# Carrying the extra tokens of a split-precision projection as trailing columns of one matmul

## The chip, the core and the metric

The kernel runs on one core of one Trainium2 chip. The metric is the device time of one launch in microseconds (us): 1000.98 us before the change, the median of 3 runs (1000.5 to 1001.47).

## What is computed

One layer of a hybrid encoder over 512 tokens with 16 learned meta tokens ahead of them, so 528 token columns. Cut to what matters here:

```python
h_res = concat([meta(16), x(512)])            # (528, 2048)
P = rmsnorm(h_res, g) @ w_in                  # w_in: 2048 x 8320
Pr, Pc = P[:, :4224], P[:, 4224:]
Pr = Pr + (shift_by_one_token(Pr) - Pr) * mu  # r, k, v, g_r and two low-rank inputs
y_a = rwkv7(r, decay, k, v, kk, a) ...        # recurrence over all 528 tokens
Bg, Cg, hc, g_c = split(Pc)
y_b = Bg * causal_conv_width3(Cg * hc) * silu(g_c)
out = rmsnorm(h_res + concat([y_a, y_b]) @ w_out)[16:]
```

The output keeps only the 512 real tokens. k and v enter the recurrence, which starts at the meta tokens, so they need all 528 columns. r, g, C and h need the 512 real tokens and the two tokens before them (token shift, convolution). B and g_c need the 512 alone.

## The kernel before, in words

Every float32 operand of the projection is split into a high and a low part of type fp32r, `x = xh + xl` and `w = hi + lo`, and a product is the sum of three matmuls: hi by xh, hi by xl, lo by xh. The tokens lie along the free dimension: `xh` and `xl` are 128 partitions by 16 slices of the 2048 inputs (`KT`) by `LX` = 576 columns, of which the first 528 hold tokens.

The projection is cut into 65 tiles of 128 output columns, in the order of `plan`: the low-rank tile, then 8 each of k, r, v, g, B, C, h and gc. A tile's weights arrive by DMA in four quarters; ScalarE rounds each to its high part (L158) and VectorE or GpSimd forms the low part (L159). `main` (L358) makes a tile with `steps` (L337): for each quarter, for each of the token ranges, for each of the quarter's 4 slices, three matmuls into one PSUM bank. The ranges are

```python
FULL = ((0, 272), (272, L))     # k, v, low-rank: 272 and 256 columns, two banks
TAIL = ((14, 272), (272, L))    # r, g, C, h: 258 and 256 columns, two banks
REAL = ((META, L),)             # B, gc: 512 columns, one bank
```

so a FULL or TAIL tile is 96 matmuls (48 of each width) and a REAL tile 48. The first four tiles (low-rank, k0, r0, B0) run interleaved while the inputs still arrive; of the tiles after them 15 are FULL (k1 to k7 and the eight v) and 31 are TAIL (r1 to r7 and the eight each of g, C and h).

A finished tile is evacuated by `scaled` (L371): VectorE multiplies each bank by `rs`, the row of RMS factors of the tokens, into an SBUF tile (`pr`, or `u` and `hh` for C and h). `shift_full` and `shift_real` then apply the token shift: ScalarE scales the tile by mu (`sh`), VectorE adds the rest.

TensorE's order is written out by hand. `mains` is a generator that yields after every matmul with a modelled time of 0.43 ns a column; `fill(ns)` emits projection matmuls until so many modelled ns have gone by, `until` emits them until a given tile is done. Between the fills stand the blocks of the recurrence's preparation: `prepare(i)` waits for k and r of head pair i, makes decay-scaled operands `ar` and `bk` on VectorE, then after `fill(FW["gram"])` the Gram matmuls (L703, and L713 for the meta chunk) that read them. `FW` is the table of these fills; `gram` holds for even i. `recur` does the same for the nine steps of the recurrence later. The other engines' order is made by a scheduler from the program's dependencies. After the projection follows the output product (L1285) in a form with seven block products, and the final norm.

Of the kernel before, what the change touches and what calls it, by code (L numbers as in the profile page):

```python
# [9 lines left out]
F32 = mybir.dt.float32  # L10
# [3 lines left out]
ALU = mybir.AluOpType  # L14
# [26 lines left out]


FW = dict(
    evac=34, start=1062, lora=2200, gram=8000, meta={0: 2000}, gram_b=13500, gram2=5500, misc=2000, v=2000, vt=1000, solve=24500, more={0: 5500, 2: 2400},
    tr=3200, lev=3000, cp=4200, out=1500, begin=19500, p=2900, u=2900, s=5200, last=3700, mix=2600,
)

# [51 lines left out]
def hymba_kernel(ctx: ExitStack, tc: tile.TileContext, xt, xtok, front, w_in, w_out, pv, lup, cst, msk, gf, out):  # L99
# [77 lines left out]
    xh = xp.tile([P, KT, LX], F32R, name="xh")  # L177
    xl = xp.tile([P, KT, LX], F32R, name="xl")
    rs = xp.tile([P, L], F32, name="rs")
    la = cq.tile([P, 2, L], F32R, name="la")  # L180
    ones = xp.tile([P, P + 2], F32R, name="ones")
    omm = xp.tile([P, 33], F32, name="omm")
# [150 lines left out]
    FULL = ((0, 272), (272, L))  # L333
    TAIL = ((14, 272), (272, L))
    REAL = ((META, L),)

    def steps(ps, ranges, k4, q, ks=range(4), rs_=range(2)):  # L337
        hi, lo = quarters[q]
# [12 lines left out]
    def banks(ranges, name, pool, tag):  # L351
        return [pool.tile([P, b - a], F32, tag=tag, name=f"ps_{name}_{r}") for r, (a, b) in enumerate(ranges)]
# [5 lines left out]
    def main(j, ranges, name):  # L358
        prefetch(2 * j + 4)
        early = state["banks"]  # L360
        state.update(tile=j, step=0, banks=[])
        ps = [early[r][:, 0 : b - a] for r, (a, b) in enumerate(ranges)] if early else banks(ranges, name, pm, "main")
        for k4 in range(4):
            if k4 == 1:
                prefetch(2 * j + 5)
            for t in steps(ps, ranges, k4, 4 * j + k4):
                state["step"] += 1
                yield t
        return ps

    def scaled(ranges, ps, dst, base):  # L371
        for (a, b), p in zip(ranges, ps):
            nc.vector.tensor_tensor(out=dst[:, a - base : b - base], in0=p, in1=rs[:, a:b], op=ALU.mult)

# [116 lines left out]
    def token_scale(yb, part):  # L491
        prs = pi.tile([P, 512], F32, tag="misc", name="prs")
        if part == 0:
            for j in range(4):
                nc.tensor.transpose(prs[:, j * P : (j + 1) * P], yb[:, j], ident)
            nc.vector.tensor_copy(rs[:, 0:512], prs)
        else:
            nc.tensor.transpose(prs[:, 0:META], yb[0:META, 4], ident[0:META, 0:META])
            nc.vector.tensor_copy(rs[:, 512:L], prs[:, 0:META])

    def mains():
        pa = banks(FULL, "lora", pm, "main")
        pb = banks(FULL, "k0", pz, "tz")
        pc = banks(TAIL, "r0", pm, "main")
        pd = [pi.tile([P, SEQ], F32, tag="ser", name="ps_B0")]
        four = ((pa, FULL), (pb, FULL), (pc, TAIL), (pd, REAL))
        for k in range(4):
            for n, (ps, rg) in enumerate(four):
                if k == n == 0:
                    hi, lo = quarters[0]  # L510
                    for ww, xx, first in ((hi, xh, True), (lo, xh, False), (hi, xl, False)):
                        for p, (a, b) in zip(ps, rg):
                            nc.tensor.matmul(p, ww[:, 0:P], xx[:, 0, a:b], start=first, stop=False)
                            yield (b - a) * 0.43
                    continue
                yield from steps(ps, rg, 0, 2 * n, (k,))
        for k4 in range(1, 4):
            for n, (ps, rg) in enumerate(four):
                h = 4 * (k4 // 2) + n
                if k4 == 2:  # L520
                    prefetch(h + 3)
                if (k4, n) == (3, 3):
                    for ks, part in ((range(1), 0), (range(1, 3), 4), (range(3, 4), None)):
                        yield from steps(ps, rg, k4, 2 * h + k4 % 2, ks)
                        if part is not None:
                            token_scale(yb, part)
                        if part == 4:
                            use("lora", 0, pa)
                            use("k", 0, pb)
                    continue  # L530
                for r in range(2 if n < 3 else 1):
                    if (k4, n, r) == (3, 1, 1):
                        yb = token_scale_sums()
                    yield from steps(ps, rg, k4, 2 * h + k4 % 2, range(4), (r,))
        use("r", 0, pc)
        use("B", 0, pd)
        for j in range(4, len(plan)):
            what, i = plan[j]
            rg = FULL if what in ("k", "v") else REAL if what in ("B", "gc") else TAIL
            ps = yield from main(j, rg, f"{what}{i}")  # L540
            if (what, i) == ("h", 0):
                state["conv"] = low[4 * j + 6]
            if what == "gc" and i < 4:
                state["split"] = low[4 * j + 4]
            use(what, i, ps)
# [1022 lines left out]
```

## Time and profile before

| | |
|---|---|
| median of 3 runs | 1000.98 us (1000.5 to 1001.47) |
| the profiled execution, its own time | 1001.71 us |
| its span on the core | 999.9 us |
| granted TensorE clock, mean | 0.997 |
| TensorE matmuls: busy, instructions | 988.3 us, 9723 |
| VectorE busy | 685.7 us |
| ScalarE busy | 394.6 us |
| GpSimd busy | 271.5 us |

The profiled execution lasted 1.8 us longer than its span, for what lies around the program. A matmul's start is recorded and its end modelled: neighbouring matmuls overlap in the records, so what a matmul costs in a stream is the distance from one start to the next, not its listed duration. In the chain of work, a row gives the start, the length and the count of a stretch of equal work.

### The profile page before, as it was taken

How to read it: one execution, taken by the hardware profiler on the slowest of the kernel's cores; microseconds unless marked ns; L12 is line 12 of the kernel's file. 1: busy time of each engine (PE TensorE's matmuls, PEld its weight loads, DVE VectorE, ACT ScalarE, POOL GpSimd, SP SyncE). 2: the span in 40 equal slices, each digit the busy share in tenths (PEclk: the TensorE clock that was granted, in tenths of full speed). 3: DMA queues.
4: the chain of work that ended last, by engine and by line, in shares of the span. 5: the costliest groups of instructions: out<-in, count | busy, mean ns of one | idle time of the engine just before them, and what ended most of it. 6: DMA issues, size and time to landing. Idle time of an engine off the chain costs nothing.

```text
span 999.9 us, 23699 instructions
## 1 busy us (share of the span) xinstructions
PE 988.3 (99%) x9723; PEld 911.6 (91%) x9723; DVE 685.7 (69%) x1247; ACT 394.6 (39%) x729; POOL 271.5 (27%) x292
## 2 busy tenths in 40 slices
PE   9999999999999999999999999999999999999996
PEld 7999999999998999998999998889889898888885
DVE  6777965588765679744669644244554697997897
ACT  7553433344313434322434322222232426546463
POOL 0122423234233424232324222223332333001001
PEclk9999999999999999999999999999999999999998
DMA  9525576555575373854274846877673688797654
GB/s 329 148 85 148 132 207 171 153 144 145 141 189 165 95 193 98 203 149 119 85 197 108 197 136 192 297 215 241 204 226 99 174 264 210 187 318 175 160 127 168
DMA packets 185036, 174.82 MB, mean 175 GB/s; under 512 B 121568, under 2 KB 142816, under 8 KB 184416
## 3 DMA queue, kind: packets, MB, share of 16 engines
q1 hardware_dynamic: 182336, 164.40, 57.2%
q0 software_dynamic: 2304, 8.39, 4.8%
q8 instruction: 76, 1.25, 0.5%
q10 hardware_dynamic: 288, 0.52, 0.1%
q14 instruction: 32, 0.26, 0.1%
HBM read 136.92 MB, written 36.35 MB: 173 GB/s over the span
## 4 chain that ended last, share of the span: by engine, by line
PE 90%; DVE 5%; DMA 2%; issue 1%; SPq 0%; ACT 0%; POOL 0%; DVEq 0%; ACTq 0%; POOLq 0%
PE ps_v L346 9%; PE ps_k L346 9%; PE ps_h L346 9%; PE ps_g L346 9%; PE ps_r L346 9%; PE ps_B L346 9%; PE ps_gc L346 9%; PE ps_C L346 8%; PE M L1285 5%; PE P L1285 2%; DVE o L1256 2%; PE g L703 2%; PE Q L1285 1%; PE zs L1048 1%; PE ps_lora L346 1%
## 5 line engine op out<-in xcount | busy, mean ns | idle before, releaser
L158 ACT CAST w<-wr 128x512 fp32r<-128x512 f32 x252 | 153.0, 619 | 285.4 <-PE ps_C L346 47.3
L159 POOL TENSOR_TENSOR w<-wr,w 128x512 fp32r<-128x512 f32 x119 | 169.1, 1422 | 346.6 <-ACT w L158 289.4
L159 DVE TENSOR_TENSOR w<-wr,w 128x512 fp32r<-128x512 f32 x133 | 98.6, 747 | 114.5 <-ACT w L158 114.2
L346 PE MATMUL ps_k<-xh,w 128*128 128x272 f32 (+1 forms) x512 | 95.3, 284 | 0.0
L346 PE MATMUL ps_v<-xh,w 128*128 128x256 f32 (+1 forms) x512 | 95.3, 284 | 0.0
L346 PE MATMUL ps_r<-xh,w 128*128 128x258 f32 (+1 forms) x512 | 94.4, 281 | 0.0
L346 PE MATMUL ps_h<-xh,w 128*128 128x256 f32 (+1 forms) x512 | 94.0, 282 | 0.0
L346 PE MATMUL ps_C<-xh,w 128*128 128x256 f32 (+1 forms) x512 | 93.1, 281 | 0.0
L346 PE MATMUL ps_g<-xh,w 128*128 128x256 f32 (+1 forms) x512 | 91.5, 280 | 0.0
L346 PE MATMUL ps_B<-xh,w 128*128 128x512 f32 x256 | 83.8, 395 | 0.0
L346 PE MATMUL ps_gc<-xh,w 128*128 128x512 f32 x256 | 81.3, 392 | 0.0
L346 PEld LDWEIGHTS ps_k<-xh,w 128*128 128x128 f32 x512 | 80.0, 188 | 0.4
L346 PEld LDWEIGHTS ps_v<-xh,w 128*128 128x128 f32 x512 | 80.0, 188 | 0.3
L346 PEld LDWEIGHTS ps_h<-xh,w 128*128 128x128 f32 x512 | 79.2, 188 | 0.7
L346 PEld LDWEIGHTS ps_r<-xh,w 128*128 128x128 f32 x512 | 79.6, 188 | 0.1
L346 PEld LDWEIGHTS ps_C<-xh,w 128*128 128x128 f32 x512 | 79.2, 188 | 0.6
L346 PEld LDWEIGHTS ps_g<-xh,w 128*128 128x128 f32 x512 | 78.7, 188 | 0.2
L346 PE MATMUL ps_k<-xl,w 128*128 128x272 f32 (+1 forms) x256 | 72.6, 284 | 0.0
L346 PE MATMUL ps_v<-xl,w 128*128 128x272 f32 (+1 forms) x256 | 72.5, 283 | 0.0
L346 PE MATMUL ps_h<-xl,w 128*128 128x258 f32 (+1 forms) x256 | 71.8, 281 | 0.5 <-issue 0.5
L346 PE MATMUL ps_g<-xl,w 128*128 128x258 f32 (+1 forms) x256 | 72.0, 281 | 0.0
L346 PE MATMUL ps_r<-xl,w 128*128 128x258 f32 (+1 forms) x256 | 72.0, 281 | 0.0
(337 smaller groups left out, 2265.3 us busy)
## 6 DMA issues: line engine op xcount, KB each, us to landing
wr<-in_w_in_dram SPq DMA_DIRECT2D x126, 512.0 KB
ct<-opd SPq DMA_DIRECT2D x64, 288.0 KB
wo<-in_w_out_dram SPq DMA_DIRECT2D x24, 512.0 KB
x<-in_w_out_dram POOLq DMA_DIRECT2D x16, 512.0 KB, 6.1
opd<-ar SPq DMA_DIRECT2D x8, 576.0 KB
opd<-gt SPq DMA_DIRECT2D x16, 288.0 KB
opd<-bt SPq DMA_DIRECT2D x64, 64.0 KB
x<-in_w_out_dram SPq DMA_DIRECT2D x8, 512.0 KB
```

The costliest lines, as they stand in the source:

```text
L158: nc.scalar.copy(hi, rq)
L159: low[q] = eng.tensor_tensor(out=lo, in0=rq, in1=hi.bitcast(F32), op=ALU.subtract).ins
L346: nc.tensor.matmul(ps[r], ww[:, w], xx[:, kt, a:b], start=(kt == 0 and n == 0), stop=(kt == KT - 1 and n == 2))
L703: nc.tensor.matmul(z[h][:, c - c0], bk[hs, c, h : h + 2, :].rearrange("p a s -> p (a s)"), ar[hs, c].rearrange("p a s -> p (a s)"), start= ...
L1048: nc.tensor.matmul(d[hs, j], w, x[hs], start=(a == 0), stop=(a == b - 1))
L1256: last = nc.vector.tensor_tensor(out=lo, in0=rq, in1=hi.bitcast(F32), op=ALU.subtract)
L1285: nc.tensor.matmul(bank[s], left(prod, jj, m, s), w, start=(jj == 0 and n == 0), stop=(jj == 7 and n == 2))
```

## The change

Two token ranges of 256 columns take the place of the two ranges of FULL and TAIL in every such tile after the first four. The tokens ahead of the 512 (16 for k and v, 2 for the others) are no longer columns of the first range. Their high and their low parts are copied once, by ScalarE, behind the 528 columns of `xh`: first the high parts of tokens 14 and 15, then their low parts, then the high and the low parts of tokens 0 to 13. The second range's matmuls read over its end into them:

| per slice of the inputs | before, FULL | after, "full" | before, TAIL | after, "tail" |
|---|---|---|---|---|
| first bank: hi·xh, hi·xl, lo·xh | 272, 272, 272 | 256, 256, 256 | 258, 258, 258 | 256, 256, 256 |
| second bank: hi·xh, hi·xl, lo·xh | 256, 256, 256 | 288, 256, 274 | 256, 256, 256 | 260, 256, 258 |
| columns in all | 1584 | 1586 | 1542 | 1542 |

A matmul of `hi` so makes hi·xh and hi·xl of an extra token in two different columns of the bank, and at the evacuation these are added: VectorE scales the extra columns into a small tile `ex` (with `rsx` or `rst`, the RMS factors in the same column order), GpSimd adds the two halves into the first columns of the destination (one addition for "tail", two for "full"). The number of matmuls, the weights and the rest of the projection stay. `FW["gram"]` goes from 8000 to 8800, which puts the Gram blocks of even head pairs seven matmuls later in TensorE's order.

```diff
-    evac=34, start=1062, lora=2200, gram=8000, meta={0: 2000}, ...
+    evac=34, start=1062, lora=2200, gram=8800, meta={0: 2000}, ...
...
+    rst = xp.tile([P, 4], F32, name="rst")
+    rsx = cq.tile([P, 2 * META], F32, name="rsx")
...
+    HALF, EX = META + SEQ // 2, 2 * META
+    WIDE = {"full": (L + EX, L, L + META + 2), "tail": (L + 4, L, L + 2)}
+
+    def copy_meta():
+        for o, x, a, b in ((0, xh, META - 2, META), (2, xl, META - 2, META), (4, xh, 0, META - 2), (META + 2, xl, 0, META - 2)):
+            nc.scalar.copy(xh[:, :, L + o : L + o + b - a], x[:, :, a:b].bitcast(F32))
+
+    def copy_scale():
+        for o, a, b in ((0, META - 2, META), (2, META - 2, META), (4, 0, META - 2), (META + 2, 0, META - 2)):
+            nc.scalar.copy(rsx[:, o : o + b - a], rs[:, a:b])
+        nc.scalar.copy(rst, rsx[:, 0:4])
+
+    def pieces(kind, ps, k4, q):
+        hi, lo = quarters[q]
+        for r in range(2):
+            a = HALF if r else META
+            ends = WIDE[kind] if r else (HALF,) * 3
+            for k in range(4):
+                kt = 4 * k4 + k
+                w = slice(k * P, (k + 1) * P)
+                for n, (ww, xx, b) in enumerate(((hi, xh, ends[0]), (hi, xl, ends[1]), (lo, xh, ends[2]))):
+                    nc.tensor.matmul(
+                        ps[r][:, 0 : b - a], ww[:, w], xx[:, kt, a:b], start=(kt == 0 and n == 0),
+                        stop=(kt == KT - 1 and n == 2), skip_group_check=True,
+                    )
+                    yield (b - a) * 0.43
...
     def scaled(ranges, ps, dst, base):
+        if len(ranges) == 2 and ps[0].shape[1] == SEQ // 2:
+            n = ps[1].shape[1] - SEQ // 2
+            e = (tp if n == 4 else cq).tile([P, n], F32, tag=f"ex{n}", name="ex", bufs=2)
+            for r, (a, b) in enumerate(((META, HALF), (HALF, L))):
+                if r:
+                    nc.vector.tensor_tensor(out=e, in0=ps[1][:, SEQ // 2 :], in1=rst if n == 4 else rsx, op=ALU.mult)
+                nc.vector.tensor_tensor(
+                    out=dst[:, a - base : b - base], in0=ps[r][:, 0 : b - a], in1=rs[:, a:b], op=ALU.mult
+                )
+            nc.gpsimd.tensor_tensor(out=dst[:, META - 2 - base : META - base], in0=e[:, 0:2], in1=e[:, 2:4], op=ALU.add)
+            if n > 4:
+                nc.gpsimd.tensor_tensor(
+                    out=dst[:, -base : META - 2 - base], in0=e[:, 4 : META + 2], in1=e[:, META + 2 : EX], op=ALU.add
+                )
+            return
...
             nc.vector.tensor_copy(rs[:, 512:L], prs[:, 0:META])
+            copy_scale()
+            copy_meta()
...
-            rg = FULL if what in ("k", "v") else REAL if what in ("B", "gc") else TAIL
+            rg = "full" if what in ("k", "v") else REAL if what in ("B", "gc") else "tail"
```

`main` is changed to take its matmuls from `pieces` where the range is one of the two names.

More of the change, by code (lines that the diff above doesn't have):

```diff
@@ L43 @@
 FW = dict(
-    evac=34, start=1062, lora=2200, gram=8000, meta={0: 2000}, gram_b=13500, gram2=5500, misc=2000, v=2000, vt=1000, solve=24500, more={0: 5500, 2: 2400},
+    evac=34, start=1062, lora=2200, gram=8800, meta={0: 2000}, gram_b=13500, gram2=5500, misc=2000, v=2000, vt=1000, solve=24500, more={0: 5500, 2: 2400},
     tr=3200, lev=3000, cp=4200, out=1500, begin=19500, p=2900, u=2900, s=5200, last=3700, mix=2600,
@@ L361, in main @@
         state.update(tile=j, step=0, banks=[])
+        kind = ranges if isinstance(ranges, str) else None
+        if kind:
+            ranges = ((META, HALF), (HALF, WIDE[kind][0]))
         ps = [early[r][:, 0 : b - a] for r, (a, b) in enumerate(ranges)] if early else banks(ranges, name, pm, "main")
@@ L365, in main @@
                 prefetch(2 * j + 5)
-            for t in steps(ps, ranges, k4, 4 * j + k4):
+            for t in pieces(kind, ps, k4, 4 * j + k4) if kind else steps(ps, ranges, k4, 4 * j + k4):
                 state["step"] += 1
```

## The prediction

> **What bounds the kernel now.** I read the head of the page first, then who TensorE waits for, then the chain of work in order of time, then single matmuls in the timeline.
>
> ```profile
> PE 988.3 (99%) x9723; PEld 911.6 (91%) x9723; DVE 685.7 (69%) x1247; ACT 394.6 (39%) x729; POOL 271.5 (27%) x292
> PE 90%; DVE 5%; DMA 2%; issue 1%; SPq 0%; ACT 0%; POOL 0%; DVEq 0%; ACTq 0%; POOLq 0%
> ```
>
> ```profile
> PE pwarm L207 <- DVE cold L204: 1.4, 1, 1.4
> PE ps_h L346 <- issue: 0.5, 1, 0.5
> PE M L1285 <- DVE o L1256: 0.4, 1, 0.4
> PE ps_lora L346 <- ACT w L247: 0.4, 1, 0.4
> ```
>
> TensorE holds 90% of the chain that ended last, and its four longest waits in the whole span are 1.4, 0.5, 0.4 and 0.4 us. So the time is the sum of the distances between matmul starts, and an edit counts by what it does to these distances. The chain of waits gives them for whole tiles (start, length, count):
>
> ```profile
> 142.20 11.20 PE ps_h L346 x96
> 380.32 11.53 PE ps_v L346 x96
> 782.71 10.88 PE ps_gc L346 x48
> 793.59 11.39 PE ps_C L346 x96
> ```
>
> The REAL tile takes 10.88 / 48 = 226.7 ns for 512 columns. The two-bank tiles mix two widths, which the timeline takes apart. Each row below is the hi·xl matmul of a slice, three matmuls after the one before (start, duration, ...):
>
> ```profile
> 142.16 0.28 PE L346 MATMUL ps_h<-xl,w 128*128 128x258 f32 x1
> ...
> 143.24 0.28 PE L346 MATMUL ps_h<-xl,w 128*128 128x258 f32 x1
> ...
> 143.59 0.28 PE L346 MATMUL ps_h<-xl,w 128*128 128x256 f32 x1
> ...
> 144.61 0.28 PE L346 MATMUL ps_h<-xl,w 128*128 128x256 f32 x1
> ```
>
> ```profile
> 380.29 0.29 PE L346 MATMUL ps_v<-xl,w 128*128 128x272 f32 x1
> ...
> 381.43 0.29 PE L346 MATMUL ps_v<-xl,w 128*128 128x272 f32 x1
> ```
>
> Nine distances each: 1.08 / 9 = 120.0 ns for 258 columns, 1.02 / 9 = 113.3 ns for 256, 1.14 / 9 = 126.7 ns for 272. The tiles agree: 48 x (120.0 + 113.3) = 11.20 us, 48 x (126.7 + 113.3) = 11.52 us. In steps of 6.67 ns these are 17 steps for 256, 18 for 258, 19 for 272 and 34 for 512. Two columns past 256 cost a whole step. A rule that fits all four is 17/16 of a step per 16 columns, rounded up to whole steps: 256 gives 17.0, 258 gives 17.1 and so 18, 272 gives 18.06 and so 19, 512 gives 34.0. That rounding is what the change works on: the columns stay the same in number, but three matmuls per slice that are rounded up become two.
>
> **TensorE, term by term.** By this rule 260 columns take 18 steps (17.3 rounded up), 288 take 20 (19.1), 274 take 19 (18.2).
>
> - Tail, per slice: before 3 x 18 + 3 x 17 = 105 steps; after 4 x 17 + 18 + 18 = 104. One step, 6.67 ns.
> - Full, per slice: before 3 x 19 + 3 x 17 = 108; after 4 x 17 + 20 + 19 = 107. One step again; if 274 should take 20, none.
> - 46 tiles x 16 slices x 6.67 ns = 4.9 us off; with no gain in the 15 full tiles 31 x 16 x 6.67 = 3.3 us.
>
> Not every 256 runs at 113.3 ns. After a foreign block some runs stay slower, and so does a whole tile (ps_C above, 11.39 against 11.20 us, 0.19 us over 48 narrow matmuls, 4 ns each):
>
> ```profile
> 84.53 0.28 PE L346 MATMUL ps_r<-xl,w 128*128 128x256 f32 x1
> ...
> 85.59 0.28 PE L346 MATMUL ps_r<-xl,w 128*128 128x256 f32 x1
> ...
> 985.91 5.91 PE L1494 MATMUL end<-home,m 128*128 128x256 f32 x48
> ```
>
> The first pair gives 1.06 / 9 = 117.8 ns, 4.5 ns more; the last row, the end of the output product, (5.91 - 0.28) / 47 = 119.8 ns. A wide matmul has nothing to lose there, a narrow one has, and the change makes 736 more narrow ones (one more per slice). I take a quarter of them to be slow, an estimate between the clean tiles and ps_C: 736 x 4.5 x 1/4 = 0.8 us. So TensorE's work falls by 4.9 - 0.8 = 4.1 us, between 2.5 (no gain in the full tiles) and 4.9 us.
>
> The Trainium skill, "TensorE: Matmul & The Clock Gate", section "Back-to-back issue gap", makes the isolated distance linear in the columns, N / 2.4 + 2.5 ns when warm. That would be 109.2 and 110.0 ns for 256 and 258, where the trace has 113.3 and 120.0; the measurement decides for the step. By the page's rule the tail tiles would gain nothing and the full ones lose two columns per slice.
>
> **Evacuation.** Prices come from the nearest small instructions (line engine op ... count | busy, mean ns | idle):
>
> ```profile
> L158 ACT CAST w<-wr 128x512 fp32r<-128x512 f32 x252 | 153.0, 619 | 285.4 <-PE ps_C L346 47.3
> L159 POOL TENSOR_TENSOR w<-wr,w 128x512 fp32r<-128x512 f32 x119 | 169.1, 1422 | 346.6 <-ACT w L158 289.4 <-issue 38.6 <-DMA opd<-bt 8.6
> L377 POOL MEMSET pr_k<- 128x1 f32 x8 | 0.8, 100 | 5.4 <-DVE r L391 5.4
> L1084 POOL TENSOR_SCALAR nv<-nv 128x8 f32<-128x8 f32 x8 | 2.7, 332 | 20.4 <-DVE nv L1083 20.0
> L596 ACT ACTIVATE tz<-tz,hv 128x16 f32<-128x16 f32 x8 | 2.2, 275 | 1.3 <-PE tz L593 1.3
> ```
>
> VectorE gets 46 products of 4 or 32 PSUM columns. The 16-column copy of `rs` out of PSUM (0.17 us, row below) is nearest: 46 x 0.17 = 7.8 us on an engine that is busy 69% of the span. GpSimd gets 31 + 2 x 15 = 61 additions of 2 or 14 columns, between 100 ns (a memset of one column) and 332 ns (8 columns read and written). I take 332, the nearer in kind: 20 us on an engine busy 27%. What matters is the new wait: ScalarE's `sh` and, behind it in ScalarE's queue, weight casts now wait for a GpSimd addition, which may stand behind a weight split of 1.42 us. The casts have room: they idle 285.4 us in all, waiting mostly for TensorE to free a weight buffer, and the splits behind the additions on GpSimd idle 346.6 us. VectorE's token shift waits for `sh`. So `ar`, `bk`, `k`, `r` may come 0.3 us later as a rule and up to 0.33 + 1.42 = 1.8 us later at worst. Who waits for them on TensorE are the Gram blocks, and the tightest is this one:
>
> ```profile
> 348.22 0.68 DVE L686 TENSOR_TENSOR ar<-r,e 128x512 f32<-128x512 f32 x1
> ```
>
> ```profile
> 350.18 0.40 PE L713 MATMUL ps_k<-ar,bk 64*128 64x16 f32 x4
> ```
>
> `ar` is done at 348.90, 1.28 us ahead of the block. `gram` at 8800 moves the block seven matmuls later, 0.8 us, which makes 2.1 us, more than the worst hop. That move costs TensorE nothing by itself: the same matmuls stand in another order, and the DMAs that SyncE issues behind the block go 0.8 us later with it. In the recurrence the step that waits for `pn` has this cover:
>
> ```profile
> 661.57 0.66 ACT L1004 ACTIVATE pn<-rz 128x256 f32<-128x256 f32 x2 [2.75 <-PE rz L996]
> ```
>
> ```profile
> 664.86 0.34 PE L1013 MATMUL rz<-pn,ct 64*64 64x64 f32 x8
> ```
>
> 664.86 - 662.23 = 2.6 us, again more than one hop. Without cover a hop would cost its 1.8 us each time. I book 0.4 us for stalls that add up where hops meet, with 0 and 1.8 us as ends.
>
> **Copies.** `copy_meta` is four ScalarE copies. In the built order they stand after the last square of the input and shortly before the weight cast of this row, which idle time precedes:
>
> ```profile
> 37.96 0.62 ACT L158 CAST w<-wr 128x512 fp32r<-128x512 f32 x1 [1.22 <-issue]
> ```
>
> 4 x 0.28 = 1.1 us fits into these 1.22 us: nothing. `copy_scale` is five more, 5 x 0.28 = 1.4 us, from the moment `rs` is whole, ahead of `sh` of the low-rank tile. The first reader on TensorE is the low-rank product of head pair 0:
>
> ```profile
> 53.06 0.17 DVE L499 COPY rs<-prs 128x16 f32<-128x16 f32 x1
> ```
>
> ```profile
> 54.48 0.74 ACT L380 ACTIVATE sh_lora<-pr_lora,pvt 128x528 f32<-128x528 f32 x1
> ...
> 57.94 0.63 ACT L411 CAST la<-lora_al 64x528 fp32r<-64x528 f32 x1
> ```
>
> ```profile
> 60.53 0.29 PE L592 MATMUL tz<-la,luh 128*128 128x272 f32 x1
> ```
>
> `la` is done at 58.57, 1.96 us ahead of use. ScalarE idled before 53.95, so of the copies about 0.7 us reach past it: hidden.
>
> **Sum.** -4.1 + 0.4 = -3.7 us. On the profiled execution that is 1001.7 - 3.7 = 998.0; the median of the runs is 0.7 us lower, so 1000.98 - 3.7 = 997.3 us.
>
> **The rivals.** The rule of steps was seen in runs of 12 equal widths. The second bank now changes its width with every matmul (260, 256, 258), which this trace shows nowhere in a settled stream. Against a price for that: ps_h above changes width eight times and still takes 11.20 us, the sum of its parts. For it: the 256s at 117.8 ns and at 119.8 ns show that a narrow matmul can lose a step to its surroundings.
>
> - The narrow matmul between two wide ones is slow, 117.8 ns throughout: 736 x 4.5 x 3/4 = 2.5 us come back. -4.1 + 2.5 + 0.4 = -1.2, so 999.8 us: no change that can be told.
> - Each change of width costs: of the second bank's three matmuls two lose a step of 6.67 ns. One step per slice is where gain turns to loss; at two, 736 x 2 x 6.67 = 9.8 us against 4.9 us, with the stalls +5.3, so 1006.3 us. This is the case on the slower side.
> - The change does nothing: cost is linear after all, from 113.3 and 226.7 at 0.443 ns a column, and 258 and 272 are dear for another reason that stays. Then the full tiles pay 15 x 16 x 2 x 0.443 = 0.2 us and the stalls 0.4: 1001.6 us. The linear rule of the skill's section above is of this kind; the trace so far speaks against it.
> - 258 and 272 are dear because of the column at which they start (14 and 0, against 272 for the 256s). Then the tail slice would be 4 x 113.3 + 115.1 + 114.2 = 682.5 ns instead of 700.0, and all slices 736 x 17.5 = 12.9 us less: 988.5 us. 272 starts in the same way as 256 in all but the number, so this is unlikely.
>
> **How the numbers follow.** The forecast 0.55, the slow narrow matmul 0.24, the paid width changes 0.14, linear 0.04, the start column 0.03. A measurement of this kernel tells about 0.2%, 2.0 us, from no change: below 999.0 is faster, above 1003.0 slower. Faster: 0.55 + 0.03, less 0.01 for the forecast's own slow edge (2.5 us off and 1.8 us of stalls), 0.57. Within: 0.24 + 0.04 less 0.01, 0.27. Slower: 0.14, and 0.02 for stalls that pile up, 0.16. The range has to hold the forecast's own spread (4.9 us off and no stall, 996.1) and reach to the slow narrow matmul and the linear case, 1001.6: 995.9 to 1001.8. The forecast's case alone would be 996.1 to 999.0.
>
> **What would show it.** In the changed kernel's chain, an undisturbed tail tile (C or h early on) should take 16 x 104 x 6.67 = 11.09 us and a full one 16 x 107 x 6.67 = 11.41. In the timeline the triples of the first bank should be 340 ns, of the second 353 in a tail tile and 373 in a full one. TensorE's waits should stay below 1 us in all behind the start. I am wrong about the steps if the second bank's triple in a tail tile is near 358 (slow narrow) or 367 (paid changes), and wrong about the cover if Gram or recurrence lines appear among TensorE's waits.

## The result, and the profile after

The changed kernel takes 1005.91 us (median of 6 runs, 1004.18 to 1006.27), the kernel before on the same chip 1001.18 us (6 runs, 1000.5 to 1001.55): a ratio of 1.0045, 95% interval 1.0032 to 1.0058. It is slower by 4.7 us, where 3.7 us less were forecast. The profiled execution of the changed kernel lasted 1006.14 us, its span 1004.0 us, against 1001.71 and 999.9 us before.

The head of the page after, the counterpart of the row that the prediction started from:

```profile
span 1004.0 us, 23849 instructions
...
PE 990.3 (99%) x9723; PEld 914.5 (91%) x9723; DVE 692.4 (69%) x1293; ACT 396.3 (39%) x738; POOL 284.7 (28%) x353
```

The matmuls are as many as before, and TensorE still bounds the kernel. VectorE has 6.7 us more work, GpSimd 13.2 us, both with room. Who TensorE waits for in the changed kernel (in total, times, longest):

```profile
PE ps_g L761 <- DVE pr_v L409: 1.9, 2, 1.2
PE pwarm L209 <- DVE cold L206: 1.4, 1, 1.4
PE zy L1100 <- issue: 1.4, 1, 1.4
PE M L1333 <- DVE o L1304: 0.4, 1, 0.4
```

The first row is new. L761 is the meta Gram block (L713 before). It writes into the two PSUM banks that the next tile will use, and waits there for VectorE's products L409 of a v tile, which free these banks. The third row (`zy`, with no releaser that the profile shows) stands at the same place as the 0.5 us of `ps_h` before. The chain of work shows the second part (start, length, count of whole tiles):

```profile
130.68 11.32 PE ps_C L359 x96
142.00 11.36 PE ps_h L359 x96
```

The prediction wanted 11.09 us for such a tile; before it was 11.20. One stretch out of `ps_h`, the hi·xl matmuls of a quarter in the second bank (the first two rows) and then in the first bank of the next quarter:

```profile
143.37 0.28 PE L359 MATMUL ps_h<-xl,w 128*128 128x256 f32 x1
...
144.44 0.28 PE L359 MATMUL ps_h<-xl,w 128*128 128x256 f32 x1
144.80 0.28 PE L359 MATMUL ps_h<-xl,w 128*128 128x256 f32 x1
...
145.85 0.28 PE L359 MATMUL ps_h<-xl,w 128*128 128x256 f32 x1
```

Nine distances each: 1.07 / 9 = 118.9 ns in the second bank (260, 256, 258), 1.05 / 9 = 116.7 ns in the first, where all are 256 and 113.3 was expected. Means of the distance by position over all slices behind the first four tiles, from the starts in the two traces (distances over 150 ns, in which a wait or another block stands, are left out):

| ns | first bank: hi·xh, hi·xl, lo·xh | second bank | per slice |
|---|---|---|---|
| TAIL before | 120.0, 120.2, 120.0 (258) | 114.8, 114.9, 114.6 (256) | 704.3 |
| "tail" after | 117.3, 116.1, 116.7 (256) | 120.8 (260), 117.9 (256), 119.1 (258) | 707.8 |
| FULL before | 126.7, 126.5, 126.7 (272) | 114.1, 113.8, 113.8 (256) | 721.5 |
| "full" after | 116.2, 115.2, 114.6 (256) | 134.8 (288), 116.1 (256), 123.3 (274) | 720.2 |

The wide matmuls cost about what was forecast (120.0, 120.0, 133.3, 126.7). The narrow ones do not: their means are 114.6 to 117.9 ns, where they were 113.8 to 114.9 before and 113.3 was expected. Added up over the 46 tiles, these distances make 522.6 us before and 523.9 us after. I call this sum the TensorE sum below.

So there are two parts: 1.4 us in the TensorE sum, and new waits of which the two at the meta Gram blocks of head pairs 5 and 7 hold most (1.19 and 0.67 us idle; the tiles behind them start 1.7 and 1.1 us later against the trace before, 2.8 us in all); the wait ahead of `zy` is 0.9 us longer than the one at its place before.

### The profile page after: what moved, and what is told of

Read it like the earlier page. It is cut to its first block, busy times and chain, and to the rows that moved or that the text cites. A ratio compares the mean times of both kernels' runs of the same rounds, so it can differ in the third digit from the quotient of the medians.

```text
span 1004.0 us, 23849 instructions
## 1 busy us (share of the span) xinstructions
PE 990.3 (99%) x9723; PEld 914.5 (91%) x9723; DVE 692.4 (69%) x1293; ACT 396.3 (39%) x738; POOL 284.7 (28%) x353
## 3 DMA queue, kind: packets, MB, share of 16 engines
q8 instruction: 76, 1.25, 0.5%
## 4 chain that ended last, share of the span: by engine, by line
PE 88%; DVE 6%; DMA 2%; POOL 1%; issue 1%; ACT 1%; SPq 0%; DVEq 0%; POOLq 0%; ACTq 0%
PE ps_h L359 9%; PE ps_gc L374 9%; PE ps_g L359 9%; PE ps_B L374 8%; PE ps_k L359 8%; PE ps_C L359 8%; PE ps_v L359 7%; PE ps_r L359 6%; PE M L1333 5%; PE P L1333 4%; PE Q L1333 2%; PE ps_k L374 1%; DVE o L1304 1%; PE g L751 1%; PE ps_r L374 1%
## 5 line engine op out<-in xcount | busy, mean ns | idle before, releaser
L359 PE MATMUL ps_h<-xh,w 128*128 128x256 f32 (+2 forms) x512 | 94.5, 283 | 0.0
L359 PE MATMUL ps_v<-xh,w 128*128 128x256 f32 (+2 forms) x512 | 94.5, 285 | 0.0
L359 PE MATMUL ps_C<-xh,w 128*128 128x256 f32 (+2 forms) x512 | 93.5, 282 | 0.0
L359 PE MATMUL ps_g<-xh,w 128*128 128x256 f32 (+2 forms) x512 | 92.0, 281 | 0.0
L359 PE MATMUL ps_k<-xh,w 128*128 128x256 f32 (+1 forms) x448 | 82.6, 286 | 0.0
L359 PE MATMUL ps_r<-xh,w 128*128 128x256 f32 (+1 forms) x448 | 82.2, 281 | 0.0
L359 PE MATMUL ps_g<-xl,w 128*128 128x256 f32 x256 | 71.9, 281 | 0.0
L359 PE MATMUL ps_h<-xl,w 128*128 128x256 f32 x256 | 71.5, 279 | 0.0
L359 PE MATMUL ps_C<-xl,w 128*128 128x256 f32 x256 | 71.5, 279 | 0.0
L359 PE MATMUL ps_v<-xl,w 128*128 128x256 f32 x256 | 71.4, 279 | 0.0
```

Source lines behind the costliest of these rows:

```text
L359: nc.tensor.matmul(ps[r][:, 0 : b - a], ww[:, w], xx[:, kt, a:b], start=(kt == 0 and n == 0), stop=(kt == KT - 1 and n == 2), skip_group_c ...
```

## The experiments

**All 256 wide.** No width changes in the two-bank tiles at all; the extra tokens are left out of the product, and the evacuation reads the first columns of the bank in their place.

```diff
-            ends = WIDE[kind] if r else (HALF,) * 3
+            ends = (L,) * 3 if r else (HALF,) * 3
...
```

> The change with the extra tokens left out of the matmuls: all six matmuls of a slice are 256 columns wide, so no width changes anywhere in these tiles; the evacuation does the same work on columns that mean nothing. Slices measured so far: tail 704.3 ns before and 707.8 after, full 721.5 and 720.2. Theory of the floor (each matmul loads its own weights, and a stream cannot go below some 117 ns a matmul for long, however narrow; the 113.3 ns runs of before lived on a lead that the wide runs ahead of them gave): 6 x 117 to 120, 702 to 720 ns a slice for both kinds, tail tiles no shorter than 11.2 us, the whole some 1002 to 1004 us. Theory of the width change (narrow matmuls are slow because the width changes with every matmul of the second bank): 6 x 113.3 = 680 ns, tail tiles of 10.9 us, 496 x 28 + 240 x 40 = 23 us less, about 983 us.

995.87 us in one run. The chain of work of this kernel:

```profile
139.98 11.30 PE ps_h L359 x96
...
414.41 11.31 PE ps_C L359 x96
...
799.08 10.90 PE ps_h L359 x96
```

11.30 / 96 = 117.7 ns without a single change of width in the tile, and 10.90 / 96 = 113.5 ns in one tile. So a narrow matmul is slow without any change of width too, and there is no floor near 118 either: the same instruction runs at either price. The granted clock is 1.00 in the slow tile at 139.98 and in the fast one at 799.08, so the clock is not the reason.

**All 224 wide.** 94 of 96 matmuls of such a tile, all but the first of each bank, cover 224 columns only; the rest of the product is left out.

```diff
+                    b = b if kt == n == 0 else a + 224
```

> As the run with 256 columns, but 47 of the 48 matmuls of each bank are only 224 columns wide (the first of a bank keeps its width); the upper tokens are left out of the sums. By 17/16 of a step per 16 columns 224 columns stream in 15 steps, 100 ns. Theory of the floor: the distance stays at 117 to 120 ns, and the tile at 11.2 to 11.5 us, as with 256 columns. Theory of the width change: 6 x 100 = 600 ns a slice, tiles of 9.6 us, about 82 us less than the changed kernel, 924 us.

1089.94 us in one run, 84 us above the changed kernel, against every expectation. Two stretches of the timeline, their hi·xl rows six and twelve matmuls apart:

```profile
150.61 0.39 PE L360 MATMUL ps_C<-xl,w 128*128 128x224 f32 x1
...
151.86 0.41 PE L360 MATMUL ps_C<-xl,w 128*128 128x224 f32 x1
```

```profile
392.55 0.27 PE L360 MATMUL ps_r<-xl,w 128*128 128x224 f32 x1
...
393.89 0.27 PE L360 MATMUL ps_r<-xl,w 128*128 128x224 f32 x1
```

The first gives 1.25 / 6 = 208 ns, the second 1.34 / 12 = 111.7 ns. What differs is the granted clock, the number behind the brackets in the view of these stretches (start:end, length, TensorE busy, clock):

```profile
150.20:153.60 3.40, 3.40 (x17) 0.50 0.40 87
392.40:403.00 10.60, 10.60 (x97) 1.00 0.16 52
```

So 208 ns is the price at half clock, and at the full clock 224 columns cost 111.7 ns: not the 100 of the rule of steps, and below the 117 to 120 of the floor. Most distances of this run (4132 of 4331 between neighbouring projection matmuls) are under 125 ns, 111.5 in the mean. The 84 us are not the price of the width. TensorE waits 86.7 us in all, against 3.1 in the kernel before, mostly for ScalarE's `tz` and for weights, and the mean granted clock is 0.96 (0.998 in the changed kernel): the trace has eleven stretches at half clock before the program's end, 3.4 to 10.2 us long, and each begins in one of TensorE's eleven waits of 3.2 us or more, or at most 1.5 us behind it. Why the other engines fell behind was not traced.

**Grouped by kind.** In each quarter the four hi·xh matmuls of a bank, then the four hi·xl, then the four lo·xh, so that the width changes a quarter as often (3 times in 12 matmuls).

```diff
-            for k in range(4):
-                kt = 4 * k4 + k
-                w = slice(k * P, (k + 1) * P)
-                for n, (ww, xx, b) in enumerate(...):
+            for n, (ww, xx, b) in enumerate(...):
+                for k in range(4):
+                    kt = 4 * k4 + k
+                    w = slice(k * P, (k + 1) * P)
```

> The change with the matmuls of a quarter and bank in the order of their kind: four times hi by xh, four times hi by xl, four times lo by xh. Same matmuls, same widths, same result, but the width changes 3 times in 12 matmuls and not 12 times. Theory of the width change: three quarters of the narrow matmuls come back to 113.3 ns, tail 699 and full 716 ns a slice, 496 x 9 + 240 x 4 = 5.4 us less than the changed kernel, about 1000.5 us. Theory of the floor: 705 to 708 and 718 to 720 ns, no difference over 1 us, about 1005.5 us.

1007.49 us, ratio to the kernel before 1.0063 (1.0046 to 1.008). Tail slices 709.3 ns, full ones 722.1: not better than the changed kernel's, though the width changes a quarter as often. This takes the last ground from the rival in which each change of width is paid.

**Weights 32 elements into their buffers.** The kernel before and the changed one place the two halves of a quarter 32 or 64 elements into their buffer, by the table `AT_32`; here all stand at 32.

```diff
-    return 32 if what in ("lora", "k", "v") or part in AT_32[what][i] else 64
+    return 32
```

> The change with all weights of the k, r, v, g, C, h and B, gc tiles placed 32 elements into their buffers (the tail tiles have 64 in most quarters, B and gc 16). A third theory, of the address: a narrow matmul is slow where the weights being loaded and the columns being read stand badly to each other in SBUF, and the tail tiles' placement was chosen for columns that started at 14. It expects the tail tiles' narrow matmuls at the 115 ns of the full tiles' first bank, 704 ns a slice, 1.9 us less, about 1004 us. Theory of the floor: tail slices stay at 705 to 710 ns, within 1 us of the changed kernel.

1004.97 us, ratio 1.0038 (1.0023 to 1.0053). Tail slices fall to 705.0 ns, the first bank to 116.1, 115.4 and 115.3, and the TensorE sum to 522.6 us, that of the kernel before. The chain of work:

```profile
141.92 11.20 PE ps_h L359 x96
268.14 11.20 PE ps_C L359 x96
...
418.86 11.41 PE ps_C L359 x96
```

Two tiles are at the 11.20 us of before and the third is worse than in the changed kernel (11.36 there). So the place of the weights moves the price of the narrow matmuls, in one direction here and in the other there.

**64 everywhere**, the counterpart (`return 64`).

> The changed kernel with all input weights but those of B and gc 64 elements into their buffers (the changed kernel: a table of 32 and 64; the run before with 32 everywhere: tail slices 705.0, full 720.6). Theory A, the place of the weights sets whether a 256-column matmul takes 113 or 118 ns: with 64 everywhere the tail slices are at 709 to 712, the full ones above 720.6, and the time is 1006 to 1009. Theory B, the place does not matter and the 705 came from another order of the blocks: tail 705 to 708, time 1005 to 1006.

1007.34 us in one run; tails 708.1 ns, full slices 725.8, the TensorE sum 525.4 us. For the full tiles the place matters clearly (720.6 with 32), for the tails the mean hardly differs from that of the table (707.8).

**The Gram due time undone.**

```diff
-    evac=34, start=1062, lora=2200, gram=8800, meta={0: 2000}, ...
+    evac=34, start=1062, lora=2200, gram=8000, meta={0: 2000}, ...
```

> The changed kernel with the one other edit undone: the due time of the even pairs' Gram blocks back from 8800 to 8000. Theory A, the stalls of TensorE ahead of the meta Gram blocks of pairs 5 and 7 (1.19 and 0.67 us idle, 2.8 us by the tile starts) come from VectorE's queue, in which the evacuation of v stands behind weight splits, so the due time of the even pairs does not matter to them: they stay within 0.5 us, slices stay at 708 (tail) and 720 (full), and the time is 1005.9 +- 0.8. Theory B, the later due time pushed the even pairs' blocks into the odd pairs' and made those stalls: they go and the time is 1003.1.

1003.16 us, ratio 1.0019 (1.001 to 1.0029). The whole list of TensorE's waits of this kernel:

```profile
PE pwarm L209 <- DVE cold L206: 1.4, 1, 1.4
PE zy L1100 <- issue: 1.1, 1, 1.1
PE M L1333 <- DVE o L1304: 0.4, 1, 0.4
PE ps_B L374 <- DVE w L159: 0.2, 1, 0.2
```

The waits at L761 are gone, with 2.7 us of the time, and the slices are as in the changed kernel (707.7, 720.4). Theory B has the outcome: without the later due time of the even pairs the odd ones do not stall. That their blocks were pushed into each other, it does not show.

**The evacuation first.** The instructions of `scaled` get the priority of the Gram masks.

```diff
+    def scaled(ranges, ps, dst, base):
+        with tc.high_priority(offset=AHEAD):
+            scaled_now(ranges, ps, dst, base)
```

> The changed kernel with the evacuation's instructions (products and additions) given the same priority as the Gram blocks' masks, ahead of the weight splits. Theory A, the banks of v are late because its products stand behind weight splits on VectorE: the idle time ahead of the meta Gram blocks of pairs 5 and 7 falls below 0.2 us each and the time is 1005.9 - 2.8 = 1003.1, slices unchanged at 708 and 720. Theory B, VectorE as a whole is late there (an 1.87 us instruction beside a GpSimd split), and what is put ahead delays the splits instead: TensorE then waits for weights, and the time stays at 1005 to 1007.

1002.66 us, ratio 1.001 (1.0001 to 1.0019), with the due time still at 8800. No wait at a Gram block is left here either: TensorE's waits are the same four as in the run before, the one for `zy` 1.2 us and the one for `o` 0.5.

So it takes two things: the later due time, and a place of v's products behind the weight splits on VectorE. Either undone removes the wait.

**Each half by itself, on the matmuls of before.** First the new evacuation alone (a product of the leading 16 or 2 columns into a small tile, GpSimd additions with zeros from there, for k, v, r and g):

```diff
     def scaled(ranges, ps, dst, base):
+        n = META - ranges[0][0]
...
+            e = (tp if n == 2 else cq).tile([P, n], F32, tag=f"ex{n}", name="ex", bufs=2)
+            nc.vector.tensor_tensor(out=e, in0=ps[0][:, 0:n], in1=rs[:, META - n : META], op=ALU.mult)
+            for (a, b), p in zip(((META, 272), (272, L)), (ps[0][:, n:], ps[1])):
+                nc.vector.tensor_tensor(out=dst[:, a - base : b - base], in0=p, in1=rs[:, a:b], op=ALU.mult)
+            nc.gpsimd.tensor_tensor(out=dst[:, META - 2 - base : META - base], in0=e[:, n - 2 : n], in1=none[:, 0:2], op=ALU.add)
...
```

> The kernel before with its matmuls and columns untouched (272 and 256, 258 and 256), and only the new way of the evacuation: for k, v, r and g tiles behind the first four, the leading 16 or 2 columns go through a product of their own into a small tile and from there by the GpSimd additions (with zeros) into the destination. The tiles of C and h keep the evacuation of before. Theory A, the extra small instructions and the GpSimd hop push VectorE's queue so that the banks of v come free late: waits of TensorE over 0.5 us ahead of the meta Gram blocks appear and the time is 1001.2 + 2.8 = 1004.0, slices at 704 and 721 as before. Theory B, the hop is covered (what the prediction booked, 0.4 us) and the stalls belong to the order that the scheduler chose for the changed matmuls: 1001.2 to 1002.0.

1002.31 us, ratio 1.0013 (1.0003 to 1.0022), 1.0 us above the 1001.34 of its chip, and no wait at a Gram block. But the TensorE sum is 523.7 us against 522.6, with the same matmuls in the same widths: the tail's 256s went from 114.7 to 115.6 ns. What the evacuation costs here, the narrow matmuls pay, not a wait. The run also puts new small tiles into SBUF, as the changed kernel does; whether the order of the work or the places of the buffers raised the price, it cannot tell.

Then the due time 8800 alone on the kernel before:

> The kernel before with the due time of the even pairs' Gram blocks at 8800 in place of 8000, and nothing else. Theory A, the later due time alone makes the stalls ahead of the meta Gram blocks of pairs 5 and 7: they appear with 0.5 us or more each and the time is 1004.0. Theory B, it takes the new evacuation as well (its small instructions and the GpSimd hop make VectorE's queue late): no such wait, 1001.3 +- 0.6.

1002.12 us, ratio 1.0012 (1.0003 to 1.0021). One wait of 0.2 us at a meta Gram block, of pair 3; the TensorE sum 523.3 us. Then both:

> Both of the changed kernel's edits around the evacuation on the matmuls of before: the new evacuation for k, v, r and g tiles (1002.3 by itself) and the due time 8800. Theory A, these two make the stalls ahead of the meta Gram blocks of pairs 5 and 7 together, whatever the matmuls are: 0.5 us or more of idle time at each, 1005.0. Theory B, the stalls need the changed matmuls' times as well, as a matter of which instruction the scheduler puts first on VectorE: no such wait, 1002.3 +- 0.8.

1003.44 us, ratio 1.0026 (1.0015 to 1.0037). TensorE's waits:

```profile
PE ps_C L725 <- DVE pr_g L379: 1.5, 1, 1.5
...
PE ps_g L348 <- DVE pr_v L379: 0.5, 1, 0.5
```

The same kind of wait, on the old matmuls, but at pair 3 and behind the products of g. With 8800 the meta block of pair 3 comes one tile later than in the trace before (it writes banks of `ps_C` in place of `ps_g`), so g's products are what frees its banks. Neither theory is met as written: the two edits make such a stall together, and which pair it meets depends on the rest.

**Widths by tile.** Weights at 32, due time 8000, and in the second bank a choice of widths for C and h. The first matmul of each second bank stays 260 wide in all of them.

```diff
+    SECOND = {
+        ("C", 0): (L, L, L), ("h", 0): (L + 4, L, L), ("C", 1): (L + 4, L + 4, L + 4), ("h", 1): (L + 4, L + 4, L),
+    }
...
+            ends = SECOND.get((what, i % 2), ends) if r else ends
```

> The changed kernel with the Gram due time of before (8000), all weights 32 elements into their buffers, and the widths of the second bank's three matmuls set by tile (the sum of the extra products is left incomplete there): C of even number 256, 256, 256; h of even number 260, 256, 256; C of odd number 260, 260, 260; h of odd number 260, 260, 256; the other tiles 260, 256, 258 as in the changed kernel. In undisturbed tiles of the run with 32 everywhere the first bank's three cost 342 ns and the second bank's three 358. Theory A, a wide matmul holds its narrow neighbours at its own pace: second bank 340 with no wide one, 356 to 360 with one, with two and with three. Theory B, each has its own price (120 and 113.3), and the 358 comes from something else in those tiles: 340, 347, 360 and 353 in the order above. Theory C, narrow ones behind other narrow ones are slow as such (117.8): 353, 356, 360, 358. The time of the whole says nothing here.

1000.78 us in one run. The three matmuls of the second bank in ns, in the four tiles of each kind, from the starts:

| wide ones | C or h tiles | mean |
|---|---|---|
| none | 353.2, 341.1, 340.8, 346.7 | 345.5 |
| one | 353.5, 353.1, 353.8, 353.2 | 353.4 |
| two | 358.8, 358.8, 357.5, 358.8 | 358.5 |
| three | 359.3, 359.9, 359.5, 359.2 | 359.5 |

```profile
141.42 11.26 PE ps_h L367 x96
268.12 11.20 PE ps_C L367 x96
279.33 11.21 PE ps_h L367 x96
417.32 10.95 PE ps_C L367 x96
```

In this order: one wide matmul in the second bank's three, three, two, none. With two wide ones the three cost nearly what they cost with three, and only tiles without any come down to 113.3 ns (two of four did, and with them their first bank: 10.95 / 96 = 114.1). With one, the two narrow ones stay at 117.4 in all four tiles. Theory B (each its own price: 340, 347, 353, 360 for none, one, two and three) is out by the tiles with two, and theory A comes nearest. The tiles with one fit none of the three: 353.4 is above B's 347 and below the 356 to 360 of A and C. They also show less than the others: their first bank, all of 256 columns, is slow as well (347 to 350 ns, against 341 to 344 in the four tiles with two wide ones), so the one wide matmul need not be the reason there.

**A combined version**: due time 8000, evacuation first, and a table of places made quarter by quarter from the runs with 32 and with 64.

```diff
 AT_32 = {
-    "C": ((),) * 6 + ((2, 3), ()),
+    "C": ((0, 2, 3), (0, 1, 2, 3), (), (), (0, 2, 3), (0, 2, 3), (1, 2, 3), (0, 2, 3)),
...
```

> The version that the runs point to: the changed kernel with the Gram due time of before (8000), the evacuation at the priority of the masks, and the place of the weights (32 or 64) chosen for each quarter of each tile as the cheaper of the two runs that had 32 and 64 everywhere; their cheaper quarters sum to 521.8 us of TensorE, against 523.9 for the changed kernel and 522.6 for the kernel before. Theory A, the three causes add up: 1003.2 (due time alone undone) - 2.1 = 1001.1 or a little below, within 0.1 per cent of the kernel before. Theory B, a quarter's price depends on the quarter before it, so that a table made from separate runs does not hold: TensorE stays at 522.6 to 523.9 and the time is 1002 to 1003.2.

1003.55 us, ratio 1.0027 (1.0017 to 1.0036), the TensorE sum 523.4 us. As theory B has it: a table put together from separate runs does not hold. That a quarter's price hangs on what ran before it is the likely reading; the run changes the due time and the evacuation too and does not show it by itself. There was also a new wait of 0.7 us for a weight cast.

**What accounts for the loss.** The changed kernel with 32 everywhere and the due time 8000:

```diff
-    return 32 if what in ("lora", "k", "v") or part in AT_32[what][i] else 64
+    return 32
...
-    ..., gram=8800, ...
+    ..., gram=8000, ...
```

> The changed kernel with two things undone or adapted and nothing else: the Gram due time of before (8000), and all input weights but those of B and gc 32 elements into their buffers in place of the table. Theory A, the loss is these two, the waits ahead of the meta Gram blocks (2.7 us by the run with 8000 alone) and a table of places that suits the old widths (1.3 us of TensorE by the run with 32 alone): TensorE's two-bank tiles sum to 522.6, and the time is 1005.9 - 2.7 - 1.3 = 1001.9, within 0.1 per cent of the kernel before. Theory B, something else of the change costs as well, or the gains do not add as in the combined version: 1003 or more.

1001.74 us, ratio 1.0008 (0.9999 to 1.0017); the TensorE sum 522.6 us. Theory A to within 0.2 us, and 0.5 us above the kernel before on the same chip, an interval that still holds no change. And the kernel before without its table (the first half of that diff):

> The kernel before with all input weights but those of B and gc 32 elements into their buffers in place of the table, and nothing else. Theory A, the table of places was worth something for the old widths only by being fitted to them: without it TensorE's two-bank tiles rise from 522.6 us to 524 or more, and the kernel before takes 1002.5 or more, so that the changed widths are no worse than the old ones where neither has a table. Theory B, 32 everywhere is as good for the old widths as for the new ones: 522.6 and 1001.2, and the changed widths cost TensorE nothing and gain nothing.

1002.74 us, ratio 1.0015 (1.0006 to 1.0024); the TensorE sum 524.4 us. Its early tail tiles, 11.20 us with the table:

```profile
142.28 11.31 PE ps_h L346 x96
269.16 11.31 PE ps_C L346 x96
```

So the kernel before owes 1.8 us of TensorE to a table fitted to its own widths. With all weights at the same place the new widths are the better ones by these 1.8 us of the sum, and by 1.0 us of the time (11 runs of each on one chip).

## Why the prediction was wrong

**TensorE bounds the kernel, and what counts are the distances.** Right; every reading above is made that way. Forecast and result lie 8.4 us apart (-3.7 and +4.7): 5.5 of them are the TensorE sum (-4.1 became +1.4) and 2.4 the stalls (0.4 became 2.8); about 0.5 is left, as much as rounding and the longer wait ahead of `zy` can make.

**The steps of the wide matmuls.** Right: 260 at 120.8 ns (forecast 120.0), 258 at 119.1 (120.0); 288 at 134.8 (133.3), 274 at 123.3 (126.7), these two 1.9 ns below the forecast together. As a rule the steps hold above 256 columns only: for 224 they give 100 ns, and the run has 111.7.

**The narrow matmuls, "736 x 4.5 x 1/4 = 0.8 us".** This step failed, and it is the one that turned the sign of the TensorE term. The forecast took the 113.3 ns of clean stretches for the price of 256 columns, and made a quarter of the additional ones slow. In fact all of the narrow ones became dearer, those of the first bank too: from 114.8 ns to between 116.1 and 117.9 in the tails, from 113.9 to between 114.6 and 116.2 in the full tiles. The TensorE sum rose by 1.4 us where 4.1 less were forecast. Against the 4.9 us of the bare count of steps that is 6.3 us: by the table of distances the narrow matmuls took 6.9 us, not 0.8, and the wide ones gave 0.6 back. The runs put two causes behind it. A narrow matmul beside two wide ones does not keep its price: such a triple costs 358.5 ns, with three wide ones 359.5, so the 6.67 ns per slice could not come. An undisturbed tail slice is 700 ns (11.20 / 16) in the new form with 32 everywhere and 700 ns in the old one: 3 x 114 + 358 against 3 x 120 + 3 x 113.3. The other is the table of places: it fits the old widths, and the changed kernel kept it. That is worth 1.3 us (523.9 to 522.6). The price of 113.3 was a property of the whole arrangement and not of the instruction. The trace before had hinted at it, with whole tiles at 11.20 and at 11.39 us and the same code. What inside TensorE makes the two prices, no run shows.

**The rivals.** "The narrow matmul between two wide ones is slow, 117.8 ns throughout" named the kind of loss, and its sign came: the second bank's three matmuls of a tail slice take 357.8 ns, near 358. But it has the loss in one matmul per slice, where all four show it, and came to 999.8 us. "Each change of width costs" gave 1006.3 us, near the measured time, by luck: the runs with one width and with grouped widths contradict its reason, and 2.8 us of the loss are waits that it does not have. The start column and the linear price are out too: three wide matmuls that start at 272 cost 359.5 / 3 = 119.8 ns each and the narrow ones of the tiles without any 340.8 / 3 = 113.6, which is 6.2 ns for four columns where the linear price gives 1.8. (Beside a slow tile of 256 columns, 353 / 3 = 117.7 ns, the difference would be 2 ns; it is the fast tiles that speak against the linear price.)

**The cover of the Gram blocks, booked at 0.4 us.** Failed: the two stalls cost 2.8 us by the tile starts, and at another place than the one that was watched. `ar` comes in time: no wait for it appears among TensorE's waits in any run. But the meta Gram block has a second condition that the prediction did not look for: the two banks that it writes have to be evacuated. How much room there was is seen from the last product of v and the meta block of pair 5, in the kernel before

```profile
392.67 0.77 DVE L373 TENSOR_TENSOR pr_v<-ps_v,rs 128x272 f32<-128x272 f32 x2
```

```profile
396.59 0.30 PE L713 MATMUL ps_g<-ar,bk 64*128 64x16 f32 x4
```

(396.59 - 393.44 = 3.15 us), in the kernel before with 8800

```profile
395.46 0.76 DVE L373 TENSOR_TENSOR pr_v<-ps_v,rs 128x272 f32<-128x272 f32 x2
```

```profile
397.64 0.30 PE L713 MATMUL ps_g<-ar,bk 64*128 64x16 f32 x4
```

(1.42 us), and in the changed kernel with 8000

```profile
394.31 0.42 DVE L409 TENSOR_TENSOR pr_v<-ps_v,rs 128x256 f32<-128x256 f32 x1
394.65 0.18 DVE L408 TENSOR_TENSOR ex<-ps_v,rsx 128x32 f32<-128x32 f32 x1
394.75 1.35 DVE L159 TENSOR_TENSOR w<-wr,w 128x512 fp32r<-128x512 f32 x1
396.02 0.41 DVE L409 TENSOR_TENSOR pr_v<-ps_v,rs 128x256 f32<-128x256 f32 x1
```

```profile
397.28 0.30 PE L761 MATMUL ps_g<-ar,bk 64*128 64x16 f32 x4
```

(397.28 - 396.43 = 0.85 us). The one takes 1.7 us of the room and the other 2.3; if the two simply add, which is an estimate, both together leave 3.15 - 4.0 = -0.9. In the changed kernel, VectorE and GpSimd and then the block:

```profile
394.25 2.97 POOL L159 TENSOR_TENSOR w<-wr,w 128x512 fp32r<-128x512 f32 x2 [2.33 <-ACT w L158]
394.40 1.69 DVE L159 TENSOR_TENSOR w<-wr,w 128x512 fp32r<-128x512 f32 x1
396.01 0.41 DVE L409 TENSOR_TENSOR pr_v<-ps_v,rs 128x256 f32<-128x256 f32 x1
396.35 1.42 DVE L159 TENSOR_TENSOR w<-wr,w 128x512 fp32r<-128x512 f32 x1
397.69 0.18 DVE L408 TENSOR_TENSOR ex<-ps_v,rsx 128x32 f32<-128x32 f32 x1
397.79 0.41 DVE L409 TENSOR_TENSOR pr_v<-ps_v,rs 128x256 f32<-128x256 f32 x1
397.95 0.20 POOL L412 TENSOR_TENSOR pr_v<-ex 128x2 f32<-128x2 f32 x1 [0.73 <-DVE ex L408]
```

```profile
396.87 0.29 PE L761 MATMUL ps_g<-ar,bk 64*128 64x16 f32 x2
398.35 0.36 PE L761 MATMUL ps_g<-ar,bk 64*128 64x16 f32 x2 [1.19 <-DVE pr_v L409]
```

A weight split of 1.69 us stands ahead of v's first product and one of 1.42 us between the two. The second half of the block waits for the second product, 1.19 us. Both run beside GpSimd splits. In the trace before, where VectorE starts first, its split takes 0.68 us and the two of GpSimd take 3.46 in place of 2.97:

```profile
392.07 0.68 DVE L159 TENSOR_TENSOR w<-wr,w 128x512 fp32r<-128x512 f32 x1
```

```profile
392.14 3.46 POOL L159 TENSOR_TENSOR w<-wr,w 128x512 fp32r<-128x512 f32 x2 [2.33 <-ACT w L158]
```

The product out of PSUM takes 0.41 us beside GpSimd too. The Trainium skill, "SBUF — State Buffer", section "SBUF: two separate sides", says that VectorE's instructions with two SBUF inputs and GpSimd's share one pair of ports, which the first to start holds to its end. These rows agree with it in who is stretched; no run here tries it alone. Why the later even block leads to this order at the odd pairs was not traced further.

**"That move costs TensorE nothing by itself."** Wrong as well: 8800 alone made the kernel before 0.12% slower, and the one new wait at a Gram block is 0.2 us. It had been counted as cover for the hop. The changed kernel at 8000 needed none.

**The hop over GpSimd.** The 61 additions take 0.26 us in the mean (0.20 to 0.39 by tile), near or below the 0.332 booked. Their waiters lose more, though within the 1.8 us of the upper end: the token shift of v5 in the changed kernel idles 0.91 us for `sh`.

```profile
398.34 0.74 ACT L426 ACTIVATE sh_v<-pr_v,pvt 128x528 f32<-128x528 f32 x1 [3.12 <-POOL pr_v L414]
...
399.11 0.90 DVE L428 SCALAR_TENSOR_TENSOR v<-pr_v,omm,sh_v 128x16 f32<-128x16 f32 x2 [0.91 <-ACT sh_v L426]
```

No wait of TensorE was found behind it: in the recurrence and at `ar` the cover held.

**The copies.** Right: the first tile behind them (v0) starts at 53.41 us, 0.34 us earlier than in the trace before.

**What is open.** How the place of the weights and the work before set a narrow matmul's price; and the wait "issue" ahead of `zy` (1.4 us, 0.5 us at that place before, 0.7 to 1.4 in the runs with the new evacuation, 0.4 and 0.5 in the two without it), which no run was made for.

## What to carry to other kernels

Count the waits of a block on all that it needs, the banks that it writes as well as the operands that it reads: the stall came from the condition that nobody watched, and two edits that were each covered used the same 3.15 us. A price that is read from clean stretches of a tuned kernel is the price in that arrangement; an edit of one matmul's width put all its neighbours at another price, and a table fitted to the old arrangement went from a gain to a loss. To judge such an edit, compare both forms without the fitted table too: there the new widths were ahead, by 1.0 us.

## What the runs showed of the hardware

At the full clock a stream of fp32r matmuls, each with its own 128 x 128 weights, takes 111.7 ns a matmul at 224 columns and 113 to 118 at 256: the 32 columns less save almost nothing. A stream of equal matmuls of 256 columns has two prices, 113.5 and 117.7 ns in whole tiles of one kernel at the same clock. The runs move the mean with the place of the weights in their buffers (the TensorE sum is 522.6 us at 32 and 525.4 at 64) and with the order of the work around it (522.6 before, 523.3 with nothing but the due time changed, one trace of each); with a wider matmul in each group of three the lower price was not seen in any of the tiles that were set up for it. In the run with 224 columns TensorE's clock was halved for 3.4 to 10.2 us in or right behind each wait of 3.2 us or more, and the distance there was nearly double (208 ns), so a distance is to be read together with the granted clock of its stretch.
